# Low parts of weights added up by a DMA on a negated high part, in a three-block transformer kernel

## The chip, the cores and the metric

The program runs on one NeuronCore of a Trainium2 chip. The metric is the device time of one execution, in microseconds (us). Five engines take part: TensorE (PE, with PEld for its weight loads), VectorE (DVE), ScalarE (ACT), GpSimd (POOL) and SyncE (SP), each with a queue of its own that is worked off in order, and 16 DMA engines that all queues share.

## What is computed

Three blocks work on 512 tokens of 1024 features, all in float32. Layer 0 is banded attention beside a pooling branch, layer 1 latent attention beside a gated recurrence, and each ends with an MLP of width 4096; block 2 has a short convolution, three kinds of sparse attention and a gated per-layer embedding. Every block is built of products with weights that are used once:

```python
def first_block(x, ...):
    for layer in range(DEPTH):
        if layer % 2 == 0:
            h = rmsnorm(x, e_norm_mix[e])
            x = x + even_mixer(h, e_w_in[e], e_sink[e], e_w_pool[e], e_pool_scale[e], e_w_out[e])
        else:
            ...
            x = x + odd_mixer(h, o_w_in[o], o_g_cq[o], o_w_uq[o], ...)
        x = x + sq_relu_mlp(rmsnorm(x, norm_mlp[layer]), w_mlp1[layer], w_mlp2[layer])
    return rmsnorm(x, final_norm)
```

## The kernel before

Activations lie with the features on the 128 partitions and the 512 tokens along the free dimension, in eight chunks. A product in float32 is made of three in float32r, PE's rounded form: each operand is split into a high part (the rounded value) and a low part (what rounding left), and `mm3` (line 776) issues high by high, low weight by high activation and high weight by low activation into one PSUM bank.

The weights come in units of up to 1024 columns, 225 loads in all. `Unit.load` (line 614) has SP load a unit into a raw tile `wr` (4 buffers). `Unit.split` (line 625) then makes the high part `wh` with `copy` and the low part `wl = wr - wh` with `tt`; each has 4 buffers (`NSPLIT`), so a unit's split can begin when PE is through with the unit four before it. PE uses a full unit in 8 blocks of 128 columns with three products each, 24 products.

Nothing is scheduled at run time. The program's order is written down once by `_Flow`, which moves a clock by PE's work and lets the chains behind it (Python generators) go on when their time has come. `_Engine` books a cost for each instruction of DVE (`V`), ACT (`S`) and POOL (`G`), and `first` (line 571) gives an instruction to the engine that would be through first. `copy` (line 581) chooses between ACT and POOL, `tt` (line 591) between DVE and POOL, each with a head start that the phase sets (`gc`, `gt`, `gw` in `_TUNE`). `pump` (line 661) starts the splits of up to three units ahead, but of later units only when ACT and DVE are not booked further than `slack` ahead. On the chip each engine then goes through its own list in order and waits on semaphores.

POOL also computes: squares of the MLP's activations (`act` in `mlp`, line 1347), sums of squares, low parts of activations, scales of probabilities, parts of the convolution (`xr_blocks`, line 1568) and of the gelu, and the powers of the norms (`powm`, line 785; tile `pw`), as well as memsets of the edges of padded tiles. The names in the rows: `wr`, `wh`, `wl` are a unit's raw, high and low tile; `hi`, `lo` an activation's parts; `uh`, `ul` those of the MLP's inner activations `ma`.

By stages, in the profiled execution: layer 0's mixer ends at about 160 us, MLP 0 runs to 515, layer 1's mixer to 740, MLP 1 to 1096, block 2 to the end. The first use of a tile of MLP 0's second matrix, for instance, is at 204 us.

Of the kernel before, what the change touches and what calls it, by code (L numbers as in the profile page):

```python
# [26 lines left out]
# ---------------------------------------------------------------- host layout  # L27
# Small parameter vectors, one column per 128 features.
# [13 lines left out]
# Constants of the shapes: identity, half rotation, rope tables, pooling counts.  # L42
# [13 lines left out]
# Weight tiles, in the order in which they are used.  # L56
# [45 lines left out]
# Blocks of 128 columns of w_in_2, in the order in which they are computed.  # L102
# [12 lines left out]
def _blk(w, cols, kcs):  # L115
    """Columns `cols` and row chunks `kcs` of w, as [128, kc, n]."""
    return w[:, cols].reshape(-1, P, len(cols))[kcs].transpose(1, 0, 2)


def _tile_of(w, blocks, kcs):  # L120
    """[128, len(blocks) * len(kcs) * 128], the blocks outermost."""
    return np.concatenate([_blk(w, b, kcs).reshape(P, -1) for b in blocks], axis=1)
# [6 lines left out]
def _layout(inp):  # L129
# [11 lines left out]
    # the first one by row chunks  # L141
# [153 lines left out]
# Bias of the choice of engines, and how far the parts of the work run ahead, by phase:  # L295
# slack: how busy the engines may be when a weight is split ahead; gc, gt, gw: head start against
# GpSimd of copies, of two-operand arithmetic and of the split of weights; low: how busy the engines
# may be when a chain of low priority goes on; lat: time from an instruction to what waits for it;
# wide: generators of the fill that go on side by side; mm, sc, tr, av: most banks of each use;
# ahead, streams: of the attention.  # L300
# [12 lines left out]
# --------------------------------------------------------------------- kernel  # L313
class _Task:
    """A chain of instructions, one stage at a time; a stage may yield the time to the next one."""
# [5 lines left out]
class _Engine:  # L321
    """An engine with an estimate of when it is through with what it was given."""
# [45 lines left out]
class _Flow:  # L368
    """Order of emission: tensor engine work moves a clock, by which the chains behind it advance."""
# [39 lines left out]
    def run(self, main, fill=None, ratio=0.0):  # L409
        """main to its end, with work of `fill` beside it."""  # L410
# [33 lines left out]
    def step(self, fill):  # L444
        """The first of the leading generators of `fill` that can move does."""
# [17 lines left out]
def _both(*gens):  # L463
    """The generators by turns."""
    live = list(gens)
    while live:
        for g in list(live):
            try:
                next(g)
                yield  # L470
            except StopIteration:
                live.remove(g)
# [7 lines left out]
class _Act:  # L480
    """hi and lo parts of a [128, T] operand."""
# [7 lines left out]
def tile_hybrid(ctx: ExitStack, tc: tile.TileContext, wt, xT, pT, prm_d, cst_d, out):  # L489
# [30 lines left out]
    # ---- PSUM banks: taken and given back in the order of emission  # L520
    # most that each use may hold; one bank is kept for each use that holds none
# [49 lines left out]
    def first(*engines):  # L571
        """The engine that would be through first."""
# [8 lines left out]
    def copy(out, src, scale=None):  # L581
        """out = src (* scale)"""
        n, ps = width(out), src.space == PSUM
        sc = 1.0 if scale is None else scale
        e = first((S, 0.06 + n / 1090.0), *(() if ps else ((G, 0.07 + n * 0.00117 + fl.gc),)))
        if e is S:
            S.activation(out, src, AF.Copy, scale=sc)
        else:
            G.tensor_scalar(out, src, sc, 1.0, op0=ALU.mult, op1=ALU.mult)

    def tt(op, out, a, b, bias=None):
        """out = a op b"""
# [3 lines left out]
        else:  # L596
            e = first((V, 0.07 + n / 960.0), (G, 0.07 + n * 0.00227 + (fl.gt if bias is None else bias)))
        e.tensor_tensor(out, a, b, op=op)

    # ---- weights: units of up to 1024 columns, loaded and split ahead of their use  # L600
# [3 lines left out]
    class Unit:  # L604
# [9 lines left out]
        def load(self):  # L614
            """The next part."""
# [9 lines left out]
        def split(self):  # L625
# [7 lines left out]
            for (c0, c1), t in zip(self.parts, self.at):  # L633
                while fl.now < t:
                    yield 0.1
                copy(self.hi[:, c0:c1], r[:, c0:c1])
                yield
                tt(ALU.subtract, self.lo[:, c0:c1], r[:, c0:c1], f(self.hi[:, c0:c1]), fl.gw)
                if c1 == self.n:
                    wl["raw"] -= 1  # L640
                yield
                self.ready = c1
# [50 lines left out]
    # ---- loads  # L693
# [34 lines left out]
    def masks(*names):  # L728
        """Chain."""
# [12 lines left out]
    def warm():  # L742
        """Products of zeros, so that the tensor engine runs at its full clock when the data comes."""
# [8 lines left out]
    # a first activation, so that its table is there when the data comes  # L752
    S.activation(nhalf[:, 0:1], onec, AF.Copy, scale=-0.5)

    # ---- helpers
    def split_ps(ps, hi, lo, scale=None):
        """Chain: hi and lo parts of ps (* scale)."""
# [18 lines left out]
    def mm3(ps, w, c, a, start, stop, m=P, bw=P, cs=slice(0, T), keep=False):  # L776
        """ps += w.T @ a, of the parts hi hi, lo hi and hi lo."""
# [12 lines left out]
    class Later:  # L790
        """A value that a chain makes."""
# [5 lines left out]
    class SumSq:  # L797
        """Sum of squares over feature chunks; `tok` gives the sums per token, [128, 4]."""
# [5 lines left out]
        def add(self, src, scale=None):  # L804
            """Chain."""
# [5 lines left out]
            elif src.space == PSUM or first((S, 0.53), (G, 1.23)) is S:  # L811
                S.activation(sq, src, AF.Square)
            else:
                G.tensor_mul(sq, src, src)
# [4 lines left out]
        def total(self):  # L819
            """Chain: the parts to one."""  # L820
# [19 lines left out]
    def rstd_c(r, ss, n):  # L840
        """Chain: r.t = (ss / n + eps) ** -0.5 per token."""
# [9 lines left out]
    def bcast_c(o, r, name="bc"):  # L851
        """Chain: o.t [128, T] = r.t [128, 4], the same in every partition."""
# [17 lines left out]
    def v_stack(z):  # L870
        """Chain; z [128 = 2 heads x 64, T] -> per head [hi | lo], tokens on partitions."""
# [17 lines left out]
    def q_stacks(z, dst, i):  # L889
        """Chain; for each 64 rows of z: the hi part on the same rows, the lo part on the others."""  # L890
# [1452 lines left out]
```

## Time and profile before

| | us |
|---|---|
| median of 3 runs | 1493.93 (1493.56 to 1495.26) |
| span of the profiled execution, first to last instruction | 1493.4 |
| PE busy | 1451.9 |
| DVE busy | 898.5 |
| ACT busy | 629.1 |
| POOL busy | 348.1 |

The profiled execution's own time is known by its span alone, which lies 0.5 us under the median. Busy time of PE is no measure of its rate, since its products overlap: in the MLPs a 512-column product takes about 390 ns from start to end and one starts every 229 ns. The share of an engine over the whole span is a mean over stages that differ, so the rows below are cut by stage.

### The profile page before, as it was taken

The numbers are of one execution on the slowest core, as the hardware profiler recorded it, in microseconds if no ns is written. First come the engines' busy times: TensorE is split into PE (matmuls) and PEld (weight loads), VectorE is DVE, ScalarE is ACT, GpSimd is POOL, SyncE is SP. The second block draws the span as 40 slices with busy tenths as digits, with TensorE's granted clock in tenths as the row PEclk, the third lists the DMA queues.
The fourth block names the chain that finished last, engine by engine and source line by source line (L and its number), as shares of the span: only waits on it lengthen the run. The fifth ranks groups of instructions, "written<-read, shape, count | busy, mean of one in ns | idle before, by whom it ended". The sixth has DMA issues, their size and how long they took to land.

```text
span 1493.4 us, 17673 instructions
## 1 busy us (share of the span) xinstructions
PE 1451.9 (97%) x6783; PEld 1176.5 (79%) x6786; DVE 898.5 (60%) x1331; ACT 629.1 (42%) x1115; POOL 348.1 (23%) x294
## 2 busy tenths in 40 slices
PE   8999999999999999599999999999999999999998
PEld 6778888888888877478888888888887888888887
DVE  7997743434334579998753333434566777668743
ACT  5676322212223365478422222212433486435743
POOL 3541110201011057742120110202011112222342
PEclk9999999999999999899999999999999999999999
DMA  6112322322333421220222332233233201134221
GB/s 232 43 53 75 111 88 98 99 92 92 99 99 101 160 88 47 71 92 29 85 92 92 99 99 90 94 99 98 87 122 111 83 29 57 59 97 128 70 72 57
DMA packets 41988, 134.05 MB, mean 90 GB/s; under 512 B 4656, under 2 KB 5168, under 8 KB 41904
## 3 DMA queue, kind: packets, MB, share of 16 engines
q1 hardware_dynamic: 41904, 132.93, 27.7%
q8 instruction: 53, 0.87, 0.2%
q14 instruction: 31, 0.25, 0.1%
HBM read 126.62 MB, written 6.29 MB: 89 GB/s over the span
## 4 chain that ended last, share of the span: by engine, by line
PE 82%; DVE 13%; issue 2%; ACT 1%; POOL 1%; DMA 0%; SPq 0%; POOLq 0%; DVEq 0%; ACTq 0%
PE mm L561 72%; PE sc L561 3%; PE av L561 3%; PE tr L565 3%; DVE sg L363 2%; DVE wl L363 2%; DVE lo L363 1%; PE tr L561 1%; DVE kl L363 1%; DVE nm L363 1%; DVE mx L363 1%; DVE q L363 1%; DVE ly L363 1%; DVE gz L363 1%; DVE pl L363 0%
## 5 line engine op out<-in xcount | busy, mean ns | idle before, releaser
L561 PE MATMUL mm<-hi,wl 128*128 128x512 f32 (+1 forms) x1276 | 503.2, 394 | 14.8 <-DVE wl L363 14.8
L561 PE MATMUL mm<-hi,wh 128*128 128x512 f32 (+1 forms) x1276 | 509.7, 399 | 3.1 <-ACT hi L363 1.9
L561 PE MATMUL mm<-lo,wh 128*128 128x512 f32 (+1 forms) x1276 | 501.3, 393 | 1.9 <-DVE lo L363 1.5
L363 ACT ACTIVATE wh<-wr 128x1024 fp32r<-128x1024 f32 (+1 forms) x204 | 211.4, 1037 | 223.3 <-PE mm L561 192.6
L561 PEld LDWEIGHTS mm<-hi,wl 128*128 128x128 f32 x1276 | 241.8, 190 | 66.3 <-DVE wl L363 17.9
L561 PEld LDWEIGHTS mm<-lo,wh 128*128 128x128 f32 x1276 | 241.6, 189 | 58.0 <-DVE lo L363 3.6
L561 PEld LDWEIGHTS mm<-hi,wh 128*128 128x128 f32 x1276 | 241.8, 190 | 56.1 <-ACT hi L363 3.0
L363 DVE TENSOR_TENSOR wl<-wr,wh 128x1024 fp32r<-128x1024 f32 (+1 forms) x216 | 271.1, 1256 | 14.9 <-ACT wh L363 14.6
L363 DVE TENSOR_TENSOR x<-x,mm 128x512 f32<-128x512 f32 x112 | 76.8, 687 | 228.2 <-PE mm L561 228.1
L363 POOL TENSOR_TENSOR ma<-ma 128x512 f32<-128x512 f32 x62 | 80.8, 1304 | 532.7 <-ACT uh L363 532.7
L561 PE MATMUL mm<-uh,wl 128*128 128x512 f32 x512 | 201.6, 394 | 0.0
L561 PE MATMUL mm<-uh,wh 128*128 128x512 f32 x512 | 201.3, 393 | 0.0
L561 PE MATMUL mm<-ul,wh 128*128 128x512 f32 x512 | 200.9, 392 | 0.0
L363 ACT ACTIVATE uh<-ma 128x512 fp32r<-128x512 f32 x64 | 40.6, 634 | 261.6 <-DVE ma L363 261.6
L363 DVE SCALAR_TENSOR_TENSOR ma<-mm,rb 128x512 f32<-128x512 f32 x64 | 44.3, 692 | 132.4 <-PE mm L561 132.3
L561 PEld LDWEIGHTS mm<-uh,wh 128*128 128x128 f32 x512 | 96.1, 188 | 22.5
L561 PEld LDWEIGHTS mm<-ul,wh 128*128 128x128 f32 x512 | 96.2, 188 | 22.1
L561 PEld LDWEIGHTS mm<-uh,wl 128*128 128x128 f32 x512 | 96.2, 188 | 21.9
L363 ACT ACTIVATE p<-sc,nm 128x512 f32<-128x512 f32 (+3 forms) x136 | 75.6, 560 | 34.3 <-DVE nm L363 27.1
L363 DVE TENSOR_TENSOR ul<-ma,uh 128x512 fp32r<-128x512 f32 x64 | 44.3, 692 | 56.0 <-POOL ma L363 56.0
L363 DVE TENSOR_TENSOR pl<-tr,ph 128x512 fp32r<-128x512 f32 (+2 forms) x108 | 65.4, 622 | 16.7 <-ACT ph L363 16.2
L363 ACT ACTIVATE ph<-tr 128x512 fp32r<-128x512 f32 (+2 forms) x108 | 58.1, 548 | 29.1 <-PE tr L565 28.5
(289 smaller groups left out, 1573.7 us busy)
## 6 DMA issues: line engine op xcount, KB each, us to landing
wr<-in_wt_dram SPq DMA_DIRECT2D x218, 512.0 KB, 3.6
x<-xs SPq DMA_DIRECT2D x16, 256.0 KB, 4.4
x<-in_xT_dram SPq DMA_DIRECT2D x8, 256.0 KB, 6.1
cst<-in_cst_dram SPq DMA_DIRECT2D x8, 256.0 KB, 5.4
xs<-x SPq DMA_DIRECT2D x8, 256.0 KB, 2.0
xs<-xr SPq DMA_DIRECT2D x8, 256.0 KB, 2.3
out_dram<-o SPq DMA_DIRECT2D x8, 256.0 KB, 2.3
wr<-in_wt_dram SPq DMA_DIRECT2D x7, 256.0 KB, 3.6
```

The lines of the kernel that those rows point to most:

```text
L363: return fn(*a, **k)
L561: PE.matmul(o, l, r, start=start, stop=stop, skip_group_check=True)
L565: PE.transpose(o, i, idn)
```

## The change

`split` now has ACT write the negated high part into `wl` first (a copy with scale -1; ACT's float32r output rounds), then lets `copy` make `wh`, and has GpSimd issue a DMA that reads the weights once more from DRAM and adds them onto `wl`. `copy` chooses between ACT and DVE, `tt` always takes DVE, and the squares of `SumSq.add`, the first term of the convolution and a step of the gelu go from POOL to DVE. POOL keeps the powers, the memsets and the 225 DMAs. The planner books 1.0 us on POOL for a DMA and lets 4.0 us pass before the unit counts as ready. Comments and docstrings are dropped as well, which shifts line numbers.

```diff
     def copy(out, src, scale=None):
         n, ps = width(out), src.space == PSUM
         sc = 1.0 if scale is None else scale
-        e = first((S, 0.06 + n / 1090.0), *(() if ps else ((G, 0.07 + n * 0.00117 + fl.gc),)))
+        e = first((S, 0.06 + n / 1090.0), *(() if ps else ((V, 0.07 + n / 1500.0 + 0.3),)))
         if e is S:
             S.activation(out, src, AF.Copy, scale=sc)
         else:
-            G.tensor_scalar(out, src, sc, 1.0, op0=ALU.mult, op1=ALU.mult)
+            V.tensor_scalar(out, src, sc, 1.0, op0=ALU.mult, op1=ALU.mult)
...
         else:
-            e = first((V, 0.07 + n / 960.0), (G, 0.07 + n * 0.00227 + (fl.gt if bias is None else bias)))
+            e = V
         e.tensor_tensor(out, a, b, op=op)
...
                 while fl.now < t:
                     yield 0.1
+                S.activation(self.lo[:, c0:c1], r[:, c0:c1], AF.Copy, scale=-1.0)
                 copy(self.hi[:, c0:c1], r[:, c0:c1])
-                yield
-                tt(ALU.subtract, self.lo[:, c0:c1], r[:, c0:c1], f(self.hi[:, c0:c1]), fl.gw)
                 if c1 == self.n:
                     wl["raw"] -= 1
                 yield
+                c = 1024 * self.i
+                nc.gpsimd.dma_start(self.lo[:, c0:c1], wt[_WT[self.name], :, c + c0:c + c1], accum_op=ALU.add)
+                G.free = max(G.free, fl.now) + 1.0
+                yield 4.0
                 self.ready = c1
...
-            elif src.space == PSUM or first((S, 0.53), (G, 1.23)) is S:
+            elif src.space == PSUM or first((S, 0.53), (V, 0.9)) is S:
                 S.activation(sq, src, AF.Square)
             else:
-                G.tensor_mul(sq, src, src)
+                V.tensor_mul(sq, src, src)
...
-                G.tensor_scalar(xc, xp[:, 0:T], PR("cw", c), PR("cb", c), op0=ALU.mult, op1=ALU.add)
+                V.tensor_scalar(xc, xp[:, 0:T], PR("cw", c), PR("cb", c), op0=ALU.mult, op1=ALU.add)
...
-                G.tensor_scalar(t, t, 0.044715, 1.0, op0=ALU.mult, op1=ALU.add)
+                V.tensor_scalar(t, t, 0.044715, 1.0, op0=ALU.mult, op1=ALU.add)
```

The built programs show how this moves the instructions. First place: ACT at the very start, where the first two units (`wr_76`, `wr_87`) come in halves of 512 columns; `hi` are the high parts of the input's chunks. Before:

```order
L363 ACTIVATE wh_130<-wr_76 128x512
L363 ACTIVATE hi_133<-x_78,prm 128x512
L363 ACTIVATE hi_138<-x_80,prm 128x512
L363 ACTIVATE wh_130<-wr_76 128x512
L363 ACTIVATE sq_147<-x_78 128x512
L363 ACTIVATE hi_154<-x_83,prm 128x512
L363 ACTIVATE hi_161<-x_85,prm 128x512
L363 ACTIVATE sq_164<-x_80 128x512
L363 ACTIVATE wh_170<-wr_87 128x512
```

And in the changed program:

```order
L363 ACTIVATE wl_131<-wr_76 128x512
L363 ACTIVATE hi_134<-x_78,prm 128x512
L363 ACTIVATE hi_139<-x_80,prm 128x512
L363 ACTIVATE sq_143<-x_78 128x512
L363 ACTIVATE hi_145<-x_83,prm 128x512
L363 ACTIVATE sq_148<-x_80 128x512
L363 ACTIVATE hi_151<-x_85,prm 128x512
L363 ACTIVATE wl_156<-wr_87 128x512
L363 ACTIVATE sq_159<-x_83 128x512
L363 ACTIVATE wl_131<-wr_76 128x512
```

ACT now writes the negated parts where it wrote the high parts, and the second half of the first unit stands behind the first half of the second one.

Second place: POOL at the start of MLP 0, around the power `pw` of its norm. Before:

```order
L363 TENSOR_TENSOR lo_1514<-ya_1474,hi_1513 128x512
L363 TENSOR_SCALAR wh_1719<-wr_1552 128x1024
L363 TENSOR_TENSOR pw_1795<-ms_1789,nhalf 128x4
L363 TENSOR_TENSOR ma_1846<-ma_1846 128x512
L363 TENSOR_TENSOR ma_1891<-ma_1891 128x512
```

And in the changed program:

```order
L642 DMA wl_1693<-in_wt_dram 128x1024
L642 DMA wl_1738<-in_wt_dram 128x1024
L363 TENSOR_TENSOR pw_1826<-ms_1820,nhalf 128x4
L642 DMA wl_1811<-in_wt_dram 128x1024
L642 DMA wl_1872<-in_wt_dram 128x1024
```

POOL's arithmetic is gone, and the power stands in a row of DMA issues, each of which waits for ACT's negated part.

Third place: DVE in MLP 0, one of its rounds. Before:

```order
L363 SCALAR_TENSOR_TENSOR ma_1979<-mm_1931,rb_1818 128x512
L363 TENSOR_TENSOR wl_1977<-wr_1802,wh_1976 128x1024
L363 TENSOR_TENSOR ul_1989<-ma_1979,uh_1988 128x512
L363 SCALAR_TENSOR_TENSOR ma_2017<-mm_1972,rb_1818 128x512
L363 TENSOR_TENSOR wl_2015<-wr_1868,wh_2014 128x1024
```

And in the changed program:

```order
L363 SCALAR_TENSOR_TENSOR ma_2008<-mm_1961,rb_1846 128x512
L363 TENSOR_TENSOR ma_2008<-ma_2008 128x512
L363 TENSOR_TENSOR ul_2023<-ma_2008,uh_2022 128x512
L363 TENSOR_SCALAR wh_2043<-wr_1880 128x1024
L363 SCALAR_TENSOR_TENSOR ma_2047<-mm_2000,rb_1846 128x512
```

DVE gives up the subtraction with two inputs and takes the copy to the high part and the square. Over the whole program it has 216 subtractions fewer, 207 copies to high parts and 62 squares `ma` more, and some 200 other instructions more; ACT makes 18 high parts where it made 204, and 225 negated parts.

## Rows read from the trace of the kernel before

**Rows 1.** The page, part 1: busy time, share of the span and instructions, by engine
```profile
PE 1451.9 (97%) x6783; PEld 1176.5 (79%) x6786; DVE 898.5 (60%) x1331; ACT 629.1 (42%) x1115; POOL 348.1 (23%) x294
```

**Rows 2.** Windows: busy time (and instructions) in each stretch, granted clock, DMA share, GB/s
```profile
0.00:160.00 160.00, 150.18 (x718) 117.83 (x719) 133.55 (x234) 99.72 (x210) 57.36 (x52) 0.99 0.32 103
160.00:515.00 355.00, 355.00 (x1542) 288.25 (x1541) 154.64 (x207) 93.25 (x113) 41.86 (x32) 1.00 0.32 101
515.00:740.00 225.00, 204.28 (x943) 164.27 (x942) 196.57 (x254) 135.32 (x246) 109.16 (x97) 0.96 0.23 73
740.00:1096.00 356.00, 356.00 (x1550) 289.70 (x1549) 154.78 (x187) 98.01 (x119) 41.94 (x32) 1.00 0.30 95
1096.00:1493.00 397.00, 386.45 (x2038) 316.44 (x2039) 258.99 (x450) 202.80 (x429) 97.75 (x81) 0.99 0.25 79
800.00:850.00 50.00, 50.00 (x218) 40.61 (x217) 18.30 (x21) 11.12 (x12) 3.86 (x3) 1.00 0.30 96
```

**Rows 3.** Waits of PE from 515 to 740 us: us in total, times, longest
```profile
PE mm L561 <- DVE wl L363: 12.5, 3, 4.5
PE tr L565 <- DVE pw L363: 2.3, 1, 2.3
```

**Rows 4.** Windows of 10 us where PE or the DMA engines stand out
```profile
10.00:20.00 10.00, 9.16 (x37) 6.60 (x36) 10.00 (x11) 9.13 (x15) 5.16 (x4) 1.00 1.03 405
560.00:570.00 10.00, 10.00 (x45) 8.16 (x44) 10.00 (x8) 8.37 (x15) 10.00 (x7) 1.00 0.11 42
600.00:610.00 10.00, 3.64 (x11) 1.91 (x9) 9.97 (x10) 2.21 (x3) 4.55 (x4) 0.80 0.16 52
```

**Rows 5.** Groups of DVE, shapes apart: busy us, mean ns, then idle before
```profile
L363 DVE TENSOR_TENSOR wl<-wr,wh 128x1024 fp32r<-128x1024 f32 x210 | 265.1, 1264 | 10.2 <-ACT wh L363 9.9
L363 DVE TENSOR_TENSOR x<-x,mm 128x512 f32<-128x512 f32 x112 | 76.8, 687 | 228.2 <-PE mm L561 228.1
L363 DVE TENSOR_TENSOR kl<-z,kh 64x512 fp32r<-64x512 f32 x20 | 21.2, 1062 | 1.0 <-ACT kh L363 0.7
L363 DVE SCALAR_TENSOR_TENSOR xc<-xp,prm,xc 128x512 f32<-128x512 f32 x12 | 11.1, 934 | 2.9 <-POOL xp L363 1.9 <-POOL xc L363 0.7
L363 DVE TENSOR_TENSOR q<-ra,q 64x512 fp32r<-64x512 f32 x8 | 9.5, 1193 | 0.2
L363 DVE SCALAR_TENSOR_TENSOR ly<-sg,gz 128x512 f32<-128x512 f32 x4 | 8.4, 2110 | 0.1
L363 DVE SCALAR_TENSOR_TENSOR sg<-sg,lt 128x512 f32<-128x512 f32 x8 | 8.3, 1052 | 0.0
```

**Rows 6.** Tile mb, its DVE casts: ns min/median/max, and forms
```profile
L363 DVE CAST mb<-cst x4: 214/416/1514, 22.8 to 179.9; 128x512 bf16<-128x512 f32 x3, 128x128 bf16<-128x128 f32 x1
```

**Rows 7.** Groups of POOL, shapes apart
```profile
L363 POOL TENSOR_TENSOR ma<-ma 128x512 f32<-128x512 f32 x62 | 80.8, 1304 | 532.7 <-ACT uh L363 532.7
L363 POOL TENSOR_TENSOR wl<-wr,wh 128x1024 fp32r<-128x1024 f32 x8 | 20.7, 2591 | 6.7 <-ACT wh L363 3.4 <-issue 2.4 <-POOL kh L363 0.7
```

**Rows 8.** Groups of ACT, shapes apart
```profile
L363 ACT ACTIVATE wh<-wr 128x1024 fp32r<-128x1024 f32 x197 | 207.0, 1052 | 220.2 <-PE mm L561 192.6 <-issue 26.4 <-DMA wr<-in_wt_dram 1.0
```

**Rows 9.** Timeline, the first low part and what it holds up
```profile
4.81 0.63 ACT L363 ACTIVATE wh<-wr 128x512 fp32r<-128x512 f32 x1 [2.60 <-DMA wr<-in_wt_dram]
5.47 0.69 DVE L363 TENSOR_TENSOR wl<-wr,wh 128x512 fp32r<-128x512 f32 x1 [4.30 <-ACT wh L363]
6.84 0.40 PE L561 MATMUL mm<-hi,wl 128*128 128x512 f32 x1
...
20.74 0.50 PE L561 MATMUL mm<-hi,wl 128*128 128x512 f32 x1 [0.89 <-DVE wl L363]
```

**Rows 10.** Tile wr, the weights' loads on SP: issue to landing
```profile
DMA to landing us min/median/max: 2.9/3.6/6.8
```

**Rows 11.** Tile wr, its issues by SP: ns min/median/max
```profile
L621 SPq DMA_DIRECT2D wr<-in_wt_dram x225: 327/328/432, 1.2 to 1440.5; - x113
```

**Rows 12.** Tile pw, its powers on POOL: ns min/median/max
```profile
L363 POOL TENSOR_TENSOR pw<-ms,nhalf x7: 697/1931/1943, 28.1 to 1486.9; 128x4 f32<-128x4 f32 x5, 128x2 f32<-128x2 f32 x2
```

## Prediction

> **What bounds the kernel now.** I read the page's engine shares first, then cut the span by stage, because the share of an engine over the whole span says nothing about a stage. PE is busy for 1451.9 us of 1493.4 [rows 1]. The stage windows show where the other 41 us lie: PE never pauses in the two MLPs (355.00 of 355.00 us, 356.00 of 356.00), but leaves 9.8 us in layer 0's mixer, 20.7 in layer 1's mixer and 10.5 in block 2 [rows 2]. So 711 us of the span are PE's own pace: 218 products in 50 us, one every 0.229 us, and a unit of 24 products every 5.5 us. There no relief of another engine can shorten anything. What can move is in the two mixers, and there DVE is the engine that is full: 133.6 of 160 us and 196.6 of 225 [rows 2], and 9.97 of 10 us at 600 us, where PE did 11 instructions against 45 at 560 [rows 4]. The waits say the same: in layer 1's mixer PE waits 12.5 us for low parts of weights, three times, up to 4.5 us [rows 3], though a low part takes DVE 1.26 us: the subtraction stands in DVE's full queue.
>
> **The change, engine by engine.** The title suggests that DVE is freed. The counts of the built programs say that it is not, because POOL's arithmetic moves to DVE at the same time. Prices: a subtraction `wl` 1.264 us, 512 columns with two inputs 0.687 us [rows 5], a half-unit subtraction 0.69 us [rows 9]. A DVE copy of a whole unit is nowhere in the trace. The casts with one input are the nearest rows: 0.214 us for 128 columns and 0.416 for 512 [rows 6], so 0.53 ns a column and 0.69 us for 1024; the other end is the two-input price, 1.26. I take 0.69.
>
> *Layer 0's mixer.* DVE loses 14 subtractions of 1024 columns and 4 of 512 (20.5 us) and gains 17 and 4 copies (13.4), 23 two-input instructions of about 512 columns (15.8) and 12 with one input (5.0): 13.7 more. Against it stands relief. Where POOL computes, DVE's two-input instructions are slow: `q<-ra` took 1.193 us instead of 0.687, 8 times, 4.0 us [rows 5]; I double this for smaller groups (an estimate) and get 6 us net, of which DVE's 83% load puts 4 on the path.
>
> *Layer 1's mixer.* DVE loses 24 and 2 subtractions (31.7) and gains 15 and 1 copies (10.8), 47 two-input instructions (32.3) and 21 with one input (8.7): 20.1 more. Relief by the rows: `xc` 12 times 0.25, `ly` 4 times 1.42, `sg` 8 times 0.37 [rows 5], 11.6 us; for smaller groups half as much again. Net 3 us, all on the path, since DVE is full there. The 12.5 us of waits for `wl` do not simply vanish: 16 of the 26 high parts now stand in the same DVE queue, and PE needs them first.
>
> *MLPs.* DVE loses 64 subtractions (80.9) and gains about 64 copies (44), 31 squares `ma` and 7 squares of the residual (26), 11 us less each; PE's pace covers all of it, and what would uncover it is a weight that comes late. *Block 2.* DVE loses 44 subtractions (55.6) and gains 47 copies (32.4), 31 two-input (21.3) and 36 one-input instructions (15.1), less 7.5 for `kl` (20 times 0.375): 6 more on an engine at 65%. I charge 2.
>
> *ACT* writes 225 negated parts at 1.05 us [rows 8] and 186 high parts fewer, 23 squares fewer: some 25 us more on 629. In layer 1's mixer it goes from 135 to about 157 of 225 us: nothing on the path.
>
> *POOL* issues 225 DMAs, each held until ACT's negated part is written, and that waits in turn for PE to free the buffer. Behind a held issue stand POOL's powers and memsets. POOL's issue is in no row: SP's takes 0.33 us [rows 11], the longest short instruction of POOL, a power, 1.94 [rows 12]; I take 1. The powers were queued behind POOL's own work of 1.3 to 2.6 us before [rows 7], so I charge nothing for the swap; at worst a power waits one unit, 5.5 us, and layer 1's two norms show 2.3 us of such a wait already [rows 3].
>
> *The DMA itself.* An adding DMA is nowhere in the trace. Low end: a plain load of a unit, 3.6 us from issue to landing; high end: two of the slowest, 13.6 [rows 10]. It lies nearest to the plain load with a second reading and POOL's issue: 3.6 + 1.6 + 1 = 6.2, and so 7.3 us from ACT's start to the landed part. With four buffers a unit may start three units ahead, 16.5 us, so in the MLPs this is covered even at the high end (14.7). It is not covered at the start. There the first low part came 0.69 us after the high part and PE used it at 6.84 us [rows 9]; now it lands at 4.81 + 0.63 + 6.2 = 11.6. The second half of this unit stands on ACT behind the next unit's first half, and all of it shares the DMA engines at their fullest, 405 GB/s and a share of 1.03 between 10 and 20 us [rows 4]. PE has 48 products of 0.229 us (11 us) to do on these two units, in four pieces that now come one by one; I put the place that was reached at 20.74 us [rows 9] at 26.7: 6 us. Between 60 and 90 us three units are split only when they are first in the order; in the built program PE has 4.3, 5.5 and 4.5 us of its own work between the freed buffer and the first use, 3 us short each. DVE is full at that time, so I charge 2 of these 8 us.
>
> *Bandwidth.* A unit's load takes 0.30 of 5.5 us, 1.65 us of all 16 engines [rows 2]. If the adding one, which reads two sources, takes twice that, load and addition fill 4.95 of 5.5 us; at the pace of the fullest window, 512 KB in 1.3 us, they fill 3.9. That is tight, but enough.
>
> The Trainium skill, in Collectives: The Full Stack, section The bandwidth ceiling, says that a summing transfer is slower not by the addition but by its second source, about half the rate of a copy; by it the addition takes 3.3 us and the sum stays as it is. No run here shows it yet.
>
> The Trainium skill's SBUF — State Buffer, section Who interferes with whom, speaks against the change: descriptors of GpSimd's DMAs are held up while DVE runs one-input copies through both of its ports. The slow two-input rows of DVE beside POOL [rows 5] agree that the two engines meet at a port. By this rule each of the 7 uncovered parts would lose up to one copy, 0.69 us, and the sum would be 5 us higher.
>
> **Sum.** Start 6, layer 0's DVE 4, its short units 2, layer 1's mixer 3, block 2 2, MLPs 0: 17 us on the profiled 1493.4, which lies 0.5 under the median. 1493.9 + 17 = **1511 us**.
>
> **Rivals.** *Faster.* POOL's 109 us of work in layer 1's mixer [rows 2] slow DVE more than I counted, and its results come at 1.3 us where DVE needs 0.69 [rows 7]. If the relief there is the double, 34 us, DVE falls below its present load and most of PE's 20.7 us go, say 18; with the 6 us at the start and the rest as counted less the same in layer 0: 1493.9 - 18 + 6 = 1482. For it: 3 waits for `wl` make 12.5 us. Against it: the high parts stay in DVE's queue. Chance 0.20. *Same.* Gain in layer 1's mixer and loss at the start cancel, within 0.2% (3 us), about what a measurement of this kernel can tell from no change: 1494, chance 0.10. *The DMA engines become the bound.* If the addition takes more than 5.5 - 1.65 = 3.85 us of the 16 engines, PE waits in every unit of the MLPs. At four times a plain load, 6.6 us, each of the 128 MLP units costs 8.25 instead of 5.5: 352 us, 1846 or more. Against it: only 0.30 of the engines' time is used now. Chance 0.10. *Late landing.* At 13.6 us the three short units lose 22 us more and the start 15: 1548, chance 0.10. *The change does not do what it says,* DVE being no freer than before, is not a rival but the forecast itself, chance 0.50.
>
> **Numbers.** Slower by over 0.2% are forecast, late landing and the DMA bound, 0.70; same 0.10; faster 0.20. The forecast's own range is 1498 to 1530: without the 0.69 us copies (at 1.26 us layer 0 and layer 1's mixer gain 10 and 9 us more) 1530, with landing as fast as a plain load 1498. The range reaches from 1478, where the faster case takes nearly all of PE's 20.7 us, to 1550, past late landing; it leaves out the DMA bound and some 0.06 at the ends.
>
> **What would show it.** Right: PE full in both MLPs at 0.229 us a product; DVE's sum near 890 us and still full at 600 us; PE's first wait for a low part near 5 us long, released by a DMA; two-input rows of DVE back at 0.69 us. Wrong: PE waits for `wl` in the MLPs, or a DMA share near 1 there (DMA bound); landing above 10 us; DVE under 180 us in layer 1's mixer (the faster case); copies `wh` at 1.2 us.

## The result, and the profile after

The changed kernel took 1532.95 us (median of 4 runs, 1532.68 to 1534.15) against 1494.6 us before (4 runs): a ratio of 1.0257, with a 95% interval of 1.0243 to 1.027. That is 38.4 us slower. 17 us were forecast: the sign was right, the size was not. The time lies 3 us past the forecast's own range (1498 to 1530); the wider range holds it only because that was carried on past the rival of a late landing.

To place the loss, three marks serve that both kernels pass with nearly the same products of PE behind them: the first product with `uh` in each MLP, and the last one in MLP 1. They stand in the view of tile `uh` (count, ns, first and last start in us). Before and after, for the stretch up to 515 us:

```profile
L561 PE MATMUL mm<-uh,wh x256: 387/392/400, 204.2 to 514.5; 128*128 128x512 f32 x128
```

```profile
L561 PE MATMUL mm<-uh,wh x209: 387/393/399, 237.4 to 514.5; 128*128 128x512 f32 x105
```

PE reaches MLP 0's second matrix at 237.4 instead of 204.2 us: 33.2 of the 38 us are lost by then, in layer 0. The same marks for every kernel of this study, each stretch as its difference to the kernel before (us, from the profiled executions). One execution's stretch scatters by some 2 us: `pin_early`, whose edit stands in block 2, has +35.3 in layer 0.

| kernel | to the first `uh` (layer 0) | to the first `uh` of MLP 1 (MLP 0, layer 1) | MLP 1 | block 2 | span |
|---|---|---|---|---|---|
| before | 204.2 | 581.3 | 309.7 | 398.2 | 1493.4 |
| changed | +33.2 | -3.2 | +0.7 | +7.1 | 1531.2 |
| first_by_dve | +27.6 | -2.9 | +0.8 | +7.1 | 1526.0 |
| six_ahead | +12.7 | -5.8 | +0.9 | +5.9 | 1507.1 |
| pin_early | +35.3 | -3.3 | +0.7 | -3.1 | 1523.0 |
| arith_only | +5.4 | +2.3 | +0.8 | -4.8 | 1497.1 |
| dma_only | +30.3 | +6.0 | +0.6 | +2.4 | 1532.7 |
| six_pin_four | +2.3 | -4.7 | +0.4 | -1.4 | 1490.0 |
| more_load | +33.3 | -2.8 | +0.6 | +6.9 | 1531.4 |
| zeros_in_waits | +31.3 | -2.6 | +1.1 | +4.7 | 1527.9 |
| before_six | +6.2 | +7.5 | 0.0 | +1.0 | 1508.1 |
| arith_six | +5.0 | +4.0 | +0.3 | -5.0 | 1497.7 |
| l1_dma | +0.1 | +3.4 | +0.3 | -1.1 | 1496.1 |
| six_pin_four_7 | +0.3 | -6.8 | -0.6 | -2.9 | 1483.4 |

The engine line of the page (as [rows 1]) and the windows cut at those stages of the changed kernel (as [rows 2]):

```profile
PE 1467.8 (96%) x6783; PEld 1187.8 (78%) x6786; DVE 858.2 (56%) x1579; ACT 649.4 (42%) x1129; POOL 212.4 (14%) x257
```

```profile
0.00:193.00 193.00, 160.51 (x716) 125.52 (x717) 129.38 (x271) 102.66 (x210) 23.13 (x37) 0.90 0.58 140
193.00:547.00 354.00, 354.00 (x1541) 288.19 (x1540) 146.49 (x246) 90.19 (x106) 58.70 (x65) 1.00 0.89 196
547.00:770.00 223.00, 207.76 (x946) 166.38 (x945) 182.21 (x313) 156.22 (x273) 25.84 (x37) 0.95 0.58 133
770.00:1126.00 356.00, 356.00 (x1547) 289.29 (x1546) 144.72 (x220) 99.08 (x117) 58.98 (x66) 1.00 0.86 190
1126.00:1531.00 405.00, 389.51 (x2041) 318.38 (x2042) 255.44 (x530) 201.24 (x423) 45.76 (x53) 0.98 0.62 140
```

PE is still never idle in the MLPs, though the DMA engines are now busy for 0.86 to 0.89 of the time. In layer 0 PE leaves 32.5 us where it left 9.8 [rows 2], the granted clock is 0.90 where it was 0.99, and DVE is no longer full: 129.4 of 193 us. So it is not DVE that PE waits for. PE's waits in this stretch say what it is (us in total, times, longest):

```profile
PE mm L561 <- DMA wl<-in_wt_dram: 21.5, 6, 6.4
PE av L561 <- DVE pl L363: 3.6, 3, 2.5
```

All six are in the timeline. Here the first two on PE, and ahead of them POOL's second and third issue, the later of which is the second half of the first unit:

```profile
11.30 1.93 POOL L642 DMA_DIRECT2D wl<-in_wt_dram  x2 [4.55 <-ACT wl L363]
...
13.81 0.80 PE L561 MATMUL mm<-hi,wl 128*128 128x512 f32 x1 [6.45 <-DMA wl<-in_wt_dram]
...
21.63 0.51 PE L561 MATMUL mm<-hi,wl 128*128 128x512 f32 x1 [2.55 <-DMA wl<-in_wt_dram]
```

The other four lie between 70 and 133 us and are alike. Here one of them on PE, then POOL's timeline of the four issues, and the landings of the tile `wl` from 60 to 140 us:

```profile
89.81 0.80 PE L561 MATMUL mm<-hi,wl 128*128 128x512 f32 x1 [4.79 <-DMA wl<-in_wt_dram]
```

```profile
62.18 0.86 POOL L642 DMA_DIRECT2D wl<-in_wt_dram  x1 [8.12 <-ACT wl L363]
...
82.00 0.86 POOL L642 DMA_DIRECT2D wl<-in_wt_dram  x1 [18.73 <-ACT wl L363]
...
103.70 0.86 POOL L642 DMA_DIRECT2D wl<-in_wt_dram  x1 [20.20 <-DVE mx L363]
...
125.42 0.86 POOL L642 DMA_DIRECT2D wl<-in_wt_dram  x1 [20.70 <-ACT wl L363]
```

```profile
L642 POOL DMA_DIRECT2D wl<-in_wt_dram x4: 860/862/865, 62.2 to 125.4; - x4
DMA to landing us min/median/max: 7.3/7.8/8.2
```

Issue at 82.00, first use at 89.81: each of these waits ends 7.3 to 8.2 us after its issue. No queue of transfers stood ahead, but the adding DMA was not alone. What POOL's issue waits for, the end of ACT's negation, also frees the raw tile (DVE's copy, its other reader, is over by then or ends at nearly the same time), and SP's next weight load waits for that tile. So two transfers of 512 KB start 0.1 to 0.3 us apart. Here ACT and SP ahead of the issue at 82.00:

```profile
80.65 1.06 ACT L363 ACTIVATE wl<-wr 128x1024 fp32r<-128x1024 f32 x1
81.73 0.33 SPq L621 DMA_DIRECT2D wr<-in_wt_dram  x1
```

Both land late. The four plain loads took 4.6 to 5.4 us, where the median before was 3.6 [rows 10]. The last three units of the changed program have their adding DMAs issued with no other transfer in flight, and these landed sooner:

```profile
L642 POOL DMA_DIRECT2D wl<-in_wt_dram x3: 865/865/865, 1489.8 to 1500.9; - x3
DMA to landing us min/median/max: 5.6/5.8/5.9
```

In `dma_only`, a run below, one of the four short units had its adding DMA issued 2.2 us after the plain load, and it landed after 5.3 us; the other three, 0.2 to 1.2 us after theirs, took 7.7 to 8.0. So some 2 us of the landing go with the plain load at its side, and the rest is the transfer's own.

Behind the waits PE runs at the lower of its two clock levels, 1.2 GHz. Three windows of the changed kernel (columns as in [rows 2]; the column ahead of the DMA share is the granted clock, and between 13.8 and 18.7 us one product follows another after 0.43 us, not 0.23):

```profile
10.00:20.00 10.00, 5.27 (x12) 3.82 (x12) 6.96 (x13) 6.58 (x12) 2.67 (x3) 0.57 1.08 324
...
90.00:100.00 10.00, 10.00 (x47) 8.20 (x48) 4.61 (x12) 4.86 (x12) 0.00 (x0) 0.81 0.01 2
...
110.00:120.00 10.00, 8.40 (x26) 6.81 (x27) 2.66 (x9) 4.17 (x11) 0.00 (x0) 0.66 0.04 8
```

Block 2's loss has one place. PE waited 5.9 us for the high part of a tile `pin`, and that for a load. SP's timeline there, and the sum of PE's waits from 1380 to 1480 us:

```profile
1409.64 0.33 SPq L621 DMA_DIRECT2D wr<-in_wt_dram  x1
1410.06 0.38 SPq L1387 DMA_DIRECT2D x<-xs  x1
1422.78 0.33 SPq L621 DMA_DIRECT2D wr<-in_wt_dram  x1
1423.21 0.87 SPq L2179 DMA_DIRECT2D pin<-in_pT_dram  x2
```

```profile
PE mm L561 <- ACT hi L363: 7.4, 2, 5.9
```

The loads of `pin` stand in SP's queue behind a weight load, which waits for a raw tile; ACT's negation of that tile came at 1421.60 and ended at 1422.65, behind the scaling of probabilities in ACT's queue. Before, `pin` was issued at 1383.2 and cost PE no wait.

### The profile page after: what moved, and what is told of

It reads as the page before. It is cut to its first block, busy times and chain, and to the rows that moved or that the text cites. A ratio compares the mean times of both kernels' runs of the same rounds, so it can differ in the third digit from the quotient of the medians.

```text
span 1531.2 us, 17929 instructions
## 1 busy us (share of the span) xinstructions
PE 1467.8 (96%) x6783; PEld 1187.8 (78%) x6786; DVE 858.2 (56%) x1579; ACT 649.4 (42%) x1129; POOL 212.4 (14%) x257
## 3 DMA queue, kind: packets, MB, share of 16 engines
q0 software_dynamic: 32400, 116.14, 43.2%
q1 hardware_dynamic: 41904, 132.93, 29.3%
## 4 chain that ended last, share of the span: by engine, by line
PE 85%; DMA 4%; issue 4%; DVE 3%; ACT 3%; POOL 0%; SPq 0%; POOLq 0%; DVEq 0%; ACTq 0%
PE mm L561 75%; PE sc L561 3%; PE av L561 3%; PE tr L565 3%; DMA wl<-in_wt_dram 3%; PE tr L561 1%; ACT p L363 1%; DVE sg L363 1%; DMA x<-xs 1%; DMA pin<-in_pT_dram 1%; DVE lo L363 1%; ACT sg L363 0%; DVE nm L363 0%; ACT wl L363 0%; DMA x<-in_xT_dram 0%
## 5 line engine op out<-in xcount | busy, mean ns | idle before, releaser
L642 POOL DMA_DIRECT2D wl<-in_wt_dram x225 | 200.8, 894 | 1252.6 <-ACT wl L363 1018.1
L363 ACT ACTIVATE wl<-wr 128x1024 fp32r<-128x1024 f32 (+1 forms) x225 | 233.5, 1039 | 232.3 <-PE mm L561 226.6
L363 DVE TENSOR_SCALAR wh<-wr 128x1024 fp32r<-128x1024 f32 (+1 forms) x207 | 141.4, 684 | 10.8 <-DMA wr<-in_wt_dram 6.8
L363 DVE TENSOR_TENSOR ma<-ma 128x512 f32<-128x512 f32 x64 | 44.3, 693 | 44.2 <-ACT uh L363 44.1
```

Source lines behind the costliest of these rows:

```text
L363: return fn(*a, **k)
L642: nc.gpsimd.dma_start(self.lo[:, c0:c1], wt[_WT[self.name], :, c + c0:c + c1], accum_op=ALU.add)
```

## The experiments

Diffs are against the changed kernel unless something else is said. In all, the ratio is to the kernel before.

### The first two units without the DMA

```diff
-                S.activation(self.lo[:, c0:c1], r[:, c0:c1], AF.Copy, scale=-1.0)
+                added = self.name != "ein2"
+                if added:
+                    S.activation(self.lo[:, c0:c1], r[:, c0:c1], AF.Copy, scale=-1.0)
                 copy(self.hi[:, c0:c1], r[:, c0:c1])
+                if not added:
+                    yield
+                    tt(ALU.subtract, self.lo[:, c0:c1], r[:, c0:c1], f(self.hi[:, c0:c1]))
...
+                if added:
```

> The changed kernel, but the two units that PE needs first (ein2, four halves) get their low part from a subtraction on DVE, as in the kernel before; all other units keep the adding DMA. Landing theory: the 12 us by which PE is behind after its first 10 us of work are the two waits of 6.45 and 2.55 us for the first landed low parts and the half clock behind them, so they go: about 1533 - 12 = 1521. Elementwise theory (the loss comes from POOL's arithmetic, which now stands on DVE and ACT): the start has 4 more subtractions on DVE and keeps its loss: 1530 to 1536.

Measured: 1526.96 us, ratio 1.0216 (1.0201 to 1.0231). 6 us came back, not 12. The timeline of PE shows where the rest went:

```profile
27.81 0.79 PE L561 MATMUL mm<-hi,wl 128*128 128x512 f32 x1 [4.28 <-DMA wl<-in_wt_dram]
```

After its first 10 us of work PE was level with the kernel before, and then stood 4.28 us at the third unit, whose adding DMA POOL issued at 17.86 us: in the changed kernel the first two waits had covered that landing. Taking away a wait moves it to the next unit that is loaded as late.

### Six units ahead

```diff
-    NRAW, NSPLIT, AHEAD = 4, 4, 3
+    NRAW, NSPLIT, AHEAD = 4, 4, 6
```

> The changed kernel, but the planner looks 6 units ahead instead of 3, so that in layer 0 the adding DMAs of four units are issued earlier (PE work between the place where the negated part can be written and the first use: over 9 us instead of 4.3, 5.5, 4.5 and 8.0). No instruction is added or taken away. Landing theory: the waits of 1.59, 4.79, 4.58 and 1.55 us and the half clock behind them go, most of the 21 us that layer 0 lost after its start: 1512 to 1518. Elementwise theory: the same work stands on DVE and ACT, so 1528 to 1536.

Measured: 1508.61 us, ratio 1.0093 (1.0078 to 1.0108): 24.3 us of the 38 by one number. Up to 193 us PE's waits for landed parts now are

```profile
PE mm L561 <- DMA wl<-in_wt_dram: 11.1, 3, 6.6
```

that is, the two of the start and one of 1.24 us. It went below the range of the landing theory; the stretch with MLP 0 and layer 1's mixer gained 2.6 us as well. Why three units were too few is read from the planner's code, not measured: `pump` looks at the first three of the order, and a unit that stays in use for long, as `wpool` does, keeps its place there.

### The loads of pin ahead of the held weight load

```diff
     fl.phase("f")
+    pins = [blk("pin"), blk("pin")]
+    for c in range(2):
+        nc.sync.dma_start(pins[c], pT[:, c, :])
...
-            t = blk("pin")
-            nc.sync.dma_start(t, pT[:, c, :])
-            go(split_to(pl[c], t))
+            go(split_to(pl[c], pins[c]))
```

> The changed kernel, but the two loads of the per-layer input (pin) are issued by SP at the start of block 2's last attention instead of behind a weight load that waits for a raw buffer. Held-load theory: the 13 us that the trace shows lost near 1429 us (waits of 5.95 and 1.47 us, then the half clock) hang on these two loads alone: about 1520. Rival (the products there wait for DVE or ACT anyway, the load is only the last of several): 1528 to 1534.

Measured: 1522.42 us, ratio 1.0188 (1.0173 to 1.0203), 10.5 us less. The view of the tile `pin` has the loads 93 us earlier, and of PE's two waits for its parts (7.4 us) 0.4 us are left; block 2 went from +7.1 to -3.1.

```profile
L2312 SPq DMA_DIRECT2D pin<-in_pT_dram x2: 423/423/423, 1329.7 to 1330.2; - x2
...
  PE mm L561: 0.4, 1
```

### The two halves of the change

`arith_only` makes all low parts by subtraction (`added = False` in the first diff). `dma_only` is the kernel before with the changed `split` alone; in effect:

```diff
+                S.activation(self.lo[:, c0:c1], r[:, c0:c1], AF.Copy, scale=-1.0)
                 copy(self.hi[:, c0:c1], r[:, c0:c1])
-                yield
-                tt(ALU.subtract, self.lo[:, c0:c1], r[:, c0:c1], f(self.hi[:, c0:c1]), fl.gw)
...
+                nc.gpsimd.dma_start(self.lo[:, c0:c1], wt[_WT[self.name], :, c + c0:c + c1], accum_op=ALU.add)
+                G.free = max(G.free, fl.now) + 1.0
+                yield 4.0
```

> The half of the change without the DMA: POOL's arithmetic stands on DVE and ACT as in the changed kernel, but all low parts are made by subtraction on DVE. Landing theory: no wait for a landing is left, so layer 0 is as in the kernel before within 5 us and the loss, if any, stands in layer 1's mixer, where DVE has 20 to 25 us more than before: 1505 to 1525 in all, below the changed kernel. Elementwise theory: layer 0 still shows most of the 33 us: 1530 to 1550.

> The other half of the change: low parts by the adding DMA, but POOL's arithmetic, its copies and the choice of engines as in the kernel before. Landing theory: the waits at the start and in layer 0 are there (leads of 5.9, 5.8 and 5.3 us of PE work against a landing of 7.3 to 8.2), some 25 to 30 us, and layer 1's mixer gains what the three waits for DVE's low parts cost (12.5 us): 1505 to 1525. Port rival (POOL cannot both compute and issue: its arithmetic of 1.3 to 2.6 us stands ahead of the issues, and landings grow past 10 us): 1530 or more, with waits for landed parts in the MLPs too.

Measured: 1500.07 us for the arithmetic alone, ratio 1.0036 (1.0021 to 1.005), and 1533.54 us for the DMA alone, ratio 1.026 (1.0245 to 1.0276). The arithmetic costs 5 us (below the range expected, as block 2 gained 4.8), the DMA 38. In layer 0 it is +5.4 against +30.3: the loss belongs to the DMA. `dma_only` came out above the landing theory's range by a place that theory had as a gain: in layer 1's mixer PE waited 9.84 us for one landed part, which is the port rival's number, though its other sign, waits in the MLPs, did not come. What holds its issue is shown by `l1_dma` below; the same products of POOL stand ahead of it here.

### Three mends together

```diff
-    NRAW, NSPLIT, AHEAD = 4, 4, 3
+    NRAW, NSPLIT, AHEAD = 4, 4, 6
...
+                added = self.name not in ("ein2", "ein0")
...
```

with the early loads of `pin`, and then with the true latency:

```diff
-                    yield 4.0
+                    yield 7.0
```

> Three mends together on the changed kernel: 6 units ahead, the early loads of pin, and subtraction on DVE for the first four units (ein2 and ein0), since with two alone the wait of 4.28 us at the third took their gain away. By the places: -24 (six ahead), -10 (pin), -11 (the start) from 1533: 1486 to 1490, under the kernel before. Rival (the gains are the same slack counted twice): 1496 or more.

> six_pin_four, but the planner lets 7.0 us pass for an adding DMA instead of 4.0, nearer to the 7.3 to 8.2 us that a landing took. If the order gains from the true latency: 1485 to 1490. If what is left does not hang on landings (in six_pin_four no wait of PE over 0.4 us was put down to one): 1490 to 1494.

Measured: 1491.16 us, ratio 0.9972 (0.9963 to 0.9982), and 1485.79 us, ratio 0.9943 (0.9928 to 0.9958). The first is 1 us above its range and under the kernel before, the second in the upper theory's range. In `six_pin_four_7` no wait of PE over 0.4 us is put down to a landing. It is faster than both kernels, by 8.3 and 47 us. Of the 10 us that its profiled execution is shorter than that of the kernel before, 6.8 stand in the stretch that holds layer 1's mixer.

### What looking ahead does by itself

`before_six` and `arith_six` are the same edit of `AHEAD` on the kernel before and on `arith_only`.

> Control: the kernel before, with the planner looking 6 units ahead instead of 3. If looking ahead helps only where something must land, it gives the kernel before at most its waits of 0.78 and 0.65 us for low parts in layer 0: 1490 to 1495. If it is a gain of its own, as large as the 24 us that it gave the changed kernel, about 1470.

> Control: POOL's arithmetic on DVE and ACT, all low parts by subtraction on DVE, 6 units ahead. Against six_pin_four (1491) it differs by the DMA and by the early loads of pin. Theory (with the landings covered the DMA costs nothing, and pays by taking subtractions off DVE where DVE is full, in layer 1's mixer): 1497 to 1502, slower than six_pin_four. Rival (the adding DMA never pays, six_pin_four owes its time to looking ahead): 1488 to 1492.

Measured: 1508.87 us, ratio 1.0097 (1.0082 to 1.0113), and 1499.2 us, ratio 1.0029 (1.0017 to 1.0041). Neither theory had the first: there the same number costs 15 us, 6.2 of them in layer 0 and 7.5 up to MLP 1. PE's waits for DVE's `vz`, `v` and `pw` rose from 6.5 to 19.7 us in it; that fits splits standing earlier in DVE's queue, but no run tests the cause. The second stayed within 1 us of `arith_only`. So looking ahead is no gain of its own. Against `arith_six`, which has nothing that must land, `six_pin_four_7` is 13 us faster, 10.8 of them in the stretch with layer 1's mixer (-6.8 against +4.0): covered, the DMA pays, and it pays in the stretch where DVE is full. The two also differ by the loads of `pin` and the 7.0 of the planner, which alone moved this stretch by 2.1.

### The DMA where DVE is full, beside POOL's arithmetic

```diff
+                added = self.name.startswith(("oin", "lru", "ukv", "uq", "oout"))
```

on the kernel before, with the negation and the DMA as in `dma_only` where `added` holds.

> The kernel before, with adding DMAs for the units of layer 1's mixer alone, the place where PE waited 12.5 us for low parts from DVE; POOL's arithmetic stays on POOL. If these waits are what bounds the place: 1483 to 1487. If DVE's other work stands behind them (the changed kernel won 12 us there and gave them back within the next 20 us of work): 1492 to 1500. If POOL's arithmetic holds the issues, as at 649.9 us of dma_only (a wait of 9.84 us): 1500 or more.

Measured: 1497.78 us, ratio 1.0024 (1.0014 to 1.0034), in the second theory's range; the rows speak for the third. PE stood 9.95 us for a landed part at 618.56 us. Its queue on POOL, and ACT's timeline of the negation that it added onto:

```profile
606.65 2.10 POOL L363 TENSOR_TENSOR sg<-sg,sg 128x512 f32<-128x512 f32 x1 [5.32 <-DVE sg L363]
608.83 0.94 POOL L363 TENSOR_SCALAR gt<-gt 128x512 f32<-128x512 f32 x1
611.53 1.26 POOL L363 TENSOR_TENSOR sg<-sg,sg 128x512 f32<-128x512 f32 x1 [1.75 <-DVE sg L363]
612.74 0.89 POOL L648 DMA_DIRECT2D wl<-in_wt_dram  x1
```

```profile
606.07 1.04 ACT L363 ACTIVATE wl<-wr 128x1024 fp32r<-128x1024 f32 x1
```

The negated part was ready at 607.1 us, the DMA was issued at 612.74, because POOL's products `sg` stand ahead of it and wait for DVE. DVE was busy for 9.94 of the 10 us from 610, so this run does not tell what PE would have waited for without the hold.

### More load on the DMA engines

```diff
+            if self.name[:2] in ("m0", "m1"):
+                more = wp.tile([P, 640], F32, tag="more", bufs=2, name=uid("wm"))
+                nc.sync.dma_start(more, wt[_WT[self.name], :, c:c + 640])
```

> The changed kernel with one more plain load of 640 columns for each of the 128 units of the MLPs, into a tile that nobody reads. By the shares of the trace a unit now takes 0.87 of 5.5 us, 4.8 us, and the added load 0.625 of 1.65 us, so 5.8. Bound theory (the share is what the DMA engines have to give): each MLP unit takes 0.3 us longer, some 40 us: 1570 or more, with waits of PE for landed parts in both MLPs. Rival (the share is not yet the bound, transfers only land later): 1531 to 1540.

Measured: 1532.72 us, ratio 1.0252 (1.0237 to 1.0267): no change. The window from 160 to 500 us of the changed kernel and of this one:

```profile
160.00:500.00 340.00, 340.00 (x1481) 276.92 (x1480) 140.74 (x240) 88.32 (x105) 56.09 (x63) 1.00 0.88 192
```

```profile
160.00:500.00 340.00, 340.00 (x1480) 276.63 (x1479) 140.66 (x240) 88.27 (x105) 56.03 (x63) 1.00 0.98 251
```

31% more bytes raised the share from 0.88 to 0.98 only, and PE lost nothing. Transfers landed a little later, as the rival said (median 8.7 us against 8.4 for the adding DMAs in this window, 8.0 against 7.0 for the plain loads of `wr`). Here the share was no measure of what was left.

### Products by zeros in the waits

```diff
         mm(ps, wh[:, :m], a.hi[:, cs], start, False, us)
+        for _ in range(zeros.get(calls[0], 0)):
+            PE.matmul(ps, zc[:, :m], zc, start=False, stop=False, skip_group_check=True)
+        calls[0] += 1
```

> The changed kernel, with products by a tile of zeros (28, 20, 20 and 20 of 512 columns in bfloat16, added to the same bank) set in front of four of PE's waits for a landed part (at 13.8, 21.6, 89.8 and 111.6 us), so that PE is not idle there. Clock theory: the granted clock stays at 1.00 behind these waits, where it was 0.57 to 0.85, and the pace that was lost behind the last three comes back: 6 to 8 us, 1525 to 1527. Rival (the lost pace has another cause, or the next landing takes it): 1531 to 1535.

Measured: 1529.32 us, ratio 1.0231 (1.0216 to 1.0246), 3.6 us less. Two of the three windows shown above, in this run:

```profile
10.00:20.00 10.00, 10.00 (x46) 5.41 (x45) 6.84 (x13) 6.60 (x12) 2.64 (x3) 1.00 1.08 329
90.00:100.00 10.00, 10.00 (x59) 8.47 (x58) 7.38 (x19) 7.88 (x20) 0.00 (x0) 1.00 0.00 0
```

The clock stayed at its higher level behind the filled waits, as the clock theory said. But only 1.9 us of it were left at the first `uh`, and the time lies between the two theories. In part the next landing took what the faster pace had won: PE was through with the twelve products between the first two waits 1.2 us sooner than in the changed kernel, and yet went on at 22.00 us only, where it had been 21.63. In part the zeros took it themselves: the first 28 of them held the product of 13.81 us until 14.73. So the clock's share may be about 1 us larger than the 1.9, but the landings are the main cause.

## Why the prediction was wrong

**Right: the bound and the prices.** PE kept its pace in the MLPs. DVE was full at the worst place of layer 1's mixer, where two windows of the changed kernel read

```profile
640.00:650.00 10.00, 2.66 (x9) 1.75 (x9) 9.81 (x17) 9.17 (x17) 1.73 (x2) 0.67 0.55 112
650.00:660.00 10.00, 9.77 (x36) 7.86 (x37) 9.95 (x18) 4.95 (x9) 0.00 (x0) 0.82 0.37 99
```

The price taken for a copy (0.69 us, between 0.53 ns a column and 1.26 us) was right, and so was the fall of the two-input rows, as these groups of DVE show beside [rows 5] (1264, 1193, 1062 and 1052 ns there):

```profile
L363 DVE TENSOR_SCALAR wh<-wr 128x1024 fp32r<-128x1024 f32 x202 | 139.2, 690 | 7.2 <-PE mm L561 3.8 <-DMA wr<-in_wt_dram 3.2
L363 DVE TENSOR_TENSOR q<-ra,q 64x512 fp32r<-64x512 f32 x8 | 5.5, 685 | 0.2
L363 DVE TENSOR_TENSOR kl<-z,kh 64x512 fp32r<-64x512 f32 x20 | 13.7, 685 | 0.4
L363 DVE SCALAR_TENSOR_TENSOR sg<-sg,lt 128x512 f32<-128x512 f32 x8 | 5.3, 686 | 0.0
```

POOL's issue took 0.86 us where 1 was taken.

**The sum, term by term.** Start 6 forecast, 11.8 measured; layer 0's DVE and its short units 6, 21.4; layer 1's mixer 3, -3.2 (with MLP 0); MLP 1 nothing, 0.7; block 2 2, 7.1. DVE's two terms were too high, which offset part of the error. By the working DVE was to gain 6 us in layer 0's mixer and 3 in layer 1's and to stay near 890, and it lost 4 and 14 (129.4 and 182.2 us against 133.6 and 196.6 [rows 2]) and came to 858. The relief was larger than counted. `arith_only` comes near the 4 and 3 us that were charged (+5.4 and +2.3), but by chance: it keeps on DVE the subtractions that the working takes off, 971.3 us of DVE in all. With the landings covered, in `six_pin_four_7`, the two stretches are +0.3 and -6.8, so the run that comes nearest to the working's conditions shows no such loss. The low end of the forecast's own range, 1498, does not follow either: only 8 us of the sum hang on a landing, which leaves 1503.

**Wrong, first: the short units.** The step was: "DVE is full at that time, so I charge 2 of these 8 us." A full DVE hid nothing: PE's list is in order, so all that stands behind the waiting product waits with it, and DVE ran out of work behind the waits: it was busy for 4.61 of the 10 us from 90 and 2.66 of those from 110. The 8 us themselves were short. Three units at a landing of 6.2 us were counted; four waited, 12.5 us in all, at 7.3 to 8.2. The 6.2 us were a fair price for an adding DMA alone (5.6 to 5.9); what was missed is the plain load that the same negation lets go. `six_ahead` gives 20.5 us back in layer 0 (33.2 less 12.7). What the 8 us beyond the waits are, the lower clock behind them or the changed order, no run separates; the same edit moves layer 0 of the kernel before by +6.2 and that of `arith_only` by -0.4. The loss lay between the forecast and the rival of the late landing (1548), with a landing between 6.2 and the high end of 13.6.

**Wrong, second: the start.** The place that was reached at 20.74 us [rows 9] was forecast at 26.7; it came at 32.5, 11.8 us late instead of 6. The first part's landing, forecast for 11.6 us, let PE go on at 13.81. The second half, issued on POOL as the second of the two from 11.30 us, let it go on at 21.63, some 9 us later, with the DMA engines at a share of 1.08. With four units by subtraction, `six_pin_four` gives the whole of it back (the same product stands at 20.33 us there); with two, `first_by_dve` has it at 27.81.

**Wrong, third: SP's queue.** Block 2 was charged 2 us and cost 7.1. Its parts: a gain from the arithmetic (-4.8 in `arith_only`) and the held loads of `pin` (10.2 us, from +7.1 to -3.1); they leave 1.7 us open. The prediction asked who waits behind POOL's held issues, but not what stands on SP behind a load whose raw tile is now freed by ACT's negation.

**The rivals.** *The DMA engines become the bound:* not here, and its sign, a share near 1 in the MLPs, was a bad one, as `more_load` shows. *Faster in layer 1's mixer:* DVE fell nearly to its sign (182.2 us, the sign was under 180), but the stretch by 3.2 us only. With the starts of PE's products of both traces side by side, in order, PE won 12 us at the former waits for low parts and gave 14 back over the next 20 us of its work, and `arith_only` shows the same without any DMA (13 won, 18 given back). From 620 to 730 us of the changed kernel PE's waits are mostly for DVE's other work (us in total, times, longest), and 4.5 us for ACT's `p`:

```profile
PE tr L565 <- DVE vz L363: 6.9, 2, 3.4
PE sc L561 <- DVE qz L363: 2.6, 1, 2.6
```

**The pages.** The queue that adds kept the engines busy for 43.2% of the span with 116.14 MB, the one of plain transfers for 29.3% with 132.93:

```profile
q0 software_dynamic: 32400, 116.14, 43.2%
q1 hardware_dynamic: 41904, 132.93, 29.3%
```

That is 1.7 times the time for a byte. The Trainium skill, Collectives: The Full Stack, section The bandwidth ceiling, gave about twice for a transfer with a second source; the trace agrees roughly. The cost lay not in this rate, by which PE lost nothing in the MLPs, but in the time to the landing. By the rule of the Trainium skill's SBUF — State Buffer, section Who interferes with whom, DVE's one-input copies would hold up the descriptors of GpSimd's DMAs, at up to 0.69 us for each uncovered part. The trace of `dma_only` speaks against a price here: its copies to the high parts stand on POOL and ACT, none on DVE, and beside a plain load issued 0.2 us ahead its adding DMAs of the short units landed after 7.7 and 8.0 us, against 7.3 to 8.2 with the copies on DVE.

## What to carry to other kernels

Work that is given from an engine to a transfer trades busy time for latency: count, at every place of the order, how much work of the bound engine lies between the moment at which the transfer can start and the first use, and price what is short of the landing in full, with the next transfer behind it. Then look through every in-order queue that the new wait holds (SP's as well), because a load that nobody thought of may stand behind it. Ask also what else the same event lets go, because two transfers that start together both land late. With six units ahead, the true latency in the planner, the first four units left to DVE and the loads of `pin` put forward, the change paid: 1485.8 us against 1494.1.

## What was not expected of the hardware

An adding DMA of 512 KB landed after 5.6 to 5.9 us with no other transfer in flight, and after 7.3 to 8.2 beside one plain load of the same size, which itself took 4.6 to 5.4 instead of a median of 3.6. Two adding DMAs of 256 KB that were alone landed after 4.1 us (`l1_dma`, issued at 599.1 us) and 4.3 (`dma_only`, at 630.5), so half the bytes took about 0.7 of the time. A share of 0.98 of the DMA engines' time left PE's stream of weights whole. And a wait of 5 us is followed by products at half pace, with a granted clock of 0.57 to 0.81 in the window, which no wait of the kernel before had brought about in layer 0 to that extent.
